# An order held by dependencies: a block kernel's small products and its projections in turn on TensorE

## Chip, cores and metric

The kernel runs on one core of a Trainium2 chip. The metric is the device time of one execution in microseconds (us). Before the change it is 761.18 us, the median of three runs (760.28 to 763.1).

## What is computed

One transformer block on 256 tokens of width 1024 with 256 context tokens, in float32. Cut to what matters here:

```python
hx, hc = modulate(x), modulate(ctx)
px, pc = hx @ w_in, hc @ w_in            # split into q, k, v, hyena, rwkv, lru, gates
att = attention(q, k, v)                 # 8 heads over 2 key/value heads
rw  = rwkv(...)                          # per head, forward and backward:
    # s = s*w - (s @ kk)[:, None]*(kk*a) + v[:, None]*k ;  y = s @ r
hy, lr = hyena(...), lru(...)
x = x + g1 * (merge(gates, att, hy, rw, lr) @ w_out)
x = x + g2 * moe(modulate(x))            # 16 experts, 2 per token
```

The recurrence `s` is what the change is about. The kernel does not step through time: it cuts the 512 tokens (context, then x) into eight chunks of 64, computes all products inside a chunk at once, inverts a triangular matrix per chunk, head and direction, and then walks over the eight chunks.

## The kernel before

The program is written with a framework that orders the work. Each engine executes its own instructions strictly in one fixed order. The program text names an engine for every instruction; at build time a scheduler, which plays the program through with estimated durations, gives each engine among its ready instructions the one that comes first in the program text. Where the text wants another order, it adds a dependency that carries no semaphore and only binds the scheduler: `after(ins, other)` (line 296). A class `_Slots` (line 252) adds such dependencies by itself, so that the first writers of all tiles that share a buffer tag come in program order.

**Projections.** `proj(tile_i, both)` (line 625) computes 128 columns of `w_in` for the x tokens (`both` false) or for context and x. SP loads 512 KB of weights into one of three `raw` buffers; ScalarE rounds each half to `whi`, VectorE subtracts to get `wlo` (`split`, line 616); TensorE accumulates into a `pj` tile (two buffers) three products for each of eight slices: 24 matmuls of 128x128 by 128x256 for x alone, 48 for both. In program order the projections behind the rwkv inputs are LX0 and LX1 (line 850), K (860), V (881), Q0 to Q3 (887), LG0 and LG1 (901); six HY projections and the gates come later.

**Units.** A unit is one direction `d` and one half `i` of the four heads: (0,0), (0,1), (1,0), (1,1) as (i,d), line 837, called units 0 to 3. `unit_keys` (line 738) starts with matmuls of 64x128 by 64x512 (tile `low`), each into an `mm` tile, and then is a chain over ScalarE, VectorE and GpSimd (tanh, scan `L`, exponentials, `kr`, `kd`) that ends in the tile `KN`. `unit_products` (line 794) is TensorE's part: for each of two heads, many 64x64 matmuls of `KN` with `kr` into two `mm` tiles, which VectorE masks into `Xs`, `QX` and (d=1) `AT1`; then eight 128x128 transposes of `KN` in two `mm` tiles, which ScalarE copies to `dn`. `mm` has three buffers (line 338), so the second head's products wait for a mask of the first head's. With d=1 a unit has more of the small products than with d=0.

Before the change all of this stands in one loop ahead of the LX projections:

```python
    for n, u in enumerate(units):
        KNs.append(unit_keys(*u))
        if n:
            unit_products(*units[n - 1], KNs[n - 1])
    unit_products(*units[-1], KNs[-1])
```

So the units come first in program order, and the scheduler puts projection matmuls (LX0, LX1, K, V) wherever a unit's next product isn't ready.

**After the units.** Line 911 on, the TT chain: VectorE transposes `Xs` in four pieces into `TT`, runs 31 steps of two dependent operations (`tq`, `TT`), and transposes back (`VA`, `VB`). It needs the masks of all four units. TensorE then makes 128 small products and the loop over eight steps (line 959), the state being carried from step to step. Attention (`attend`, line 1175), the HY projections, the lru and the first gates (`gate`, line 1229) lie around it, the remaining gates and the merge after it, then the experts.

Of the kernel before, what the change touches and what calls it, by code (L numbers as in the profile page):

```python
# [76 lines left out]
def _consts():  # L77
# [101 lines left out]
T_Q, T_K, T_V, T_HY, T_R, T_RK, T_RV, T_W1, T_A1, T_G1, T_LG, T_LX, T_GT = (  # L179
    0, 4, 5, 6, 12, 14, 16, 18, 19, 20, 21, 23, 25)  # L180
# [112 lines left out]
def body(ctx, tc, I, out, dbg=None, upto=None):  # L293
    nc = tc.nc

    def after(ins, other):
        tc.add_manual_dep(ins.ins, other.ins.name, mybir.DependencyInfo(
            mybir.DependencyClass.NoSync, mybir.DependencyReason.SCHED_ONLY), reason="loads in order")
# [4 lines left out]
    V, A, G, T, SP = (_Eng(e, slots) for e in (nc.vector, nc.scalar, nc.gpsimd, nc.tensor, nc.sync))  # L303
# [36 lines left out]
    def pj():  # L340
        return pj_("pj")

    def mm():
        return mm_("mm")
# [4 lines left out]
    def act(o, i, f=AF.Copy, **k):  # L349
        A.activation(out=o, in_=i, func=f, **k)  # L350

    def stt(o, a, s, b, op0=mul, op1=add, eng=V):
        return eng.scalar_tensor_tensor(out=o, in0=a, scalar=s, in1=b, op0=op0, op1=op1)
# [16 lines left out]
    def mmul(o, l, r, start=True, stop=True, shared=False):  # L370
        return T.matmul(out=o, lhsT=l, rhs=r, start=start, stop=stop, skip_group_check=shared)

    def small(name, shape, bufs=1, p_=cw, dt=F32):
        return slots.tile(p_, [P] + shape, dt, name, name, bufs)
# [5 lines left out]
    ident = small("ident", [128], 1, cp)  # L380
# [11 lines left out]
    def pc(name):  # L392
        o, n = _PV[name]
        return pv[:, o:o + n]
# [9 lines left out]
    def tr(o, i):  # L404
        T.transpose(out=o, in_=i, identity=ident[:i.shape[0], :i.shape[0]])
# [51 lines left out]
    def rawt():  # L457
        return slots.tile(wr_, [P, 1024], F32, "raw", "raw", RAW)
# [70 lines left out]
    hcx = [[slots.tile(hx if s_ else keep, [P, 8, 256], F32R, f"h{s_}{q}", f"h{s_}{q}", 1) for q in range(2)] for s_ in range(2)]  # L529
# [10 lines left out]
    for k in range(2):  # L540
        ada_first(k)
        for j in range(4 * k, 4 * k + 4):
            for s_ in range(2):
                v = 1 - s_
                hi, lo = hcx[s_][0][:, j], hcx[s_][1][:, j]
# [66 lines left out]

    spectrum(0)


    def split(w, hf):

        hi = slots.tile(wp, [P, 512], F32R, "whi", "whi", HI)
        lo = slots.tile(wp, [P, 512], F32R, "wlo", "wlo", HI)
        w = w[:, hf * 512:hf * 512 + 512]  # L620
        act(hi, w)
        tt(lo, w, hi.bitcast(F32), sub)
        return hi, lo

    def proj(tile_i, both):

        w = rawt()
        SP.dma_start(w, I["w_in"][tile_i])
        p = pj()
        for hf in range(2):  # L630
            hi, lo = split(w, hf)
            for s_ in ((0, 1) if both else (1,)):
                o = p[:, s_ * 256:(s_ + 1) * 256] if both else p[:, 0:256]
                for jj in range(4):
                    j = 4 * hf + jj
                    ws = slice(jj * 128, (jj + 1) * 128)

                    mmul(o, hi[:, ws], hcx[s_][0][:, j], j == 0 and s_ == (0 if both else 1), False, both)
                    mmul(o, hi[:, ws], hcx[s_][1][:, j], False, False, both)
                    mmul(o, lo[:, ws], hcx[s_][0][:, j], False, j == 7, both)  # L640
        return p if both else p[:, 0:256]


# [76 lines left out]
    def natural(src, name, big, psa, n=4):  # L720
        o = big(name).rearrange("p (a c) -> p a c", a=4)
        pb = psa()
        for a in range(n):
            tr(pb[:, a * 128:(a + 1) * 128], src[:, a * 128:(a + 1) * 128])
        act(o.rearrange("p a c -> p (a c)"), pb)
        return o

    Vn = b4("Vn").rearrange("p a b -> p (a b)").rearrange("p (t i c) -> p t i c", t=4, i=2)
    for i in range(2):
        pb = mm()  # L730
# [60 lines left out]
        stt(KN4[:, :, 1:3], four(ta), -0.5, four(E3), mul, mul)  # L791
        return KN

    def unit_products(i, d, KN):
        for h in range(2):
            hs = slice(64 * h, 64 * h + 64)
            m = 16 * d + 8 * i + 4 * h
            pc_, px_ = mm(), mm()
            for c8 in range(8):
                c = c8 % 2  # L800
                vs, us = slice(64 * c, 64 * c + 64), slice(64 - 64 * c, 128 - 64 * c)
                kd_, nb_ = (KN[hs, (2 * c8 + q) * 64:(2 * c8 + q) * 64 + 64] for q in (c, 1 - c))
                Kc = Kt(d, i, c8)[hs]
                if c8 < 4:
                    o = slice(c8 * 64, c8 * 64 + 64)
                    mmul(pc_[vs, o], kd_, Kc)
                    mmul(pc_[us, o], *((Kc, nb_) if d else (nb_, Kc)))
                else:
                    k0 = 256 + (c8 - 4) * 128
                    o = slice((c8 - 4) * 128, (c8 - 4) * 128 + 128)  # L810
                    KRc = KR[d][i][hs, k0:k0 + 128]
                    mmul(px_[vs, o], kd_, KRc)
                    if d:
                        mmul(px_[us, o.start:o.start + 64], Kc, nb_)
                        mmul(px_[us, o.start + 64:o.stop], nb_, KRc[:, 64:])
                    else:
                        mmul(px_[us, o], nb_, KRc)
                if d:
                    mmul(pc_[us, 256 + (c8 // 2) * 32:288 + (c8 // 2) * 32], nb_, Kc[:, :32])
            mk = cn(f"mask{d}").rearrange("p (c t) -> p c t", c=2).unsqueeze(1).to_broadcast([P, 2, 2, 64])  # L820
            p4 = px_.rearrange("p (t c q s) -> p t c q s", t=2, c=2, q=2)
            tt(Xs[:, m:m + 2], pc_[:, :256].rearrange("p (t c s) -> p t c s", t=2, c=2), mk)
            tt(Xs[:, m + 2:m + 4], p4[:, :, :, 0], mk)
            if d:
                tt(AT1[:, m - 16:m - 12], pc_[:, 256:384].rearrange("p (t s) -> p t s", t=4),
                   cn("late1").unsqueeze(1).to_broadcast([P, 4, 32]))
            tt(QX[:, d, h, i], px_.rearrange("p (c q s) -> p c q s", c=4, q=2)[:, :, 1],
               cn(f"inc{d}").unsqueeze(1).to_broadcast([P, 4, 64]))
        dn = DN[d][i] = b4("dn").rearrange("p a b -> p (a b)").rearrange("p (c k) -> p c k", c=8)
        for c2 in range(2):  # L830
            pb = mm()
            for c4 in range(4):
                o = (4 * c2 + c4) * 128
                tr(pb[:, c4 * 128:c4 * 128 + 128], KN[:, o:o + 128])
            act(dn[:, 4 * c2:4 * c2 + 4].rearrange("p c k -> p (c k)"), pb)

    units = [(0, 0), (0, 1), (1, 0), (1, 1)]
    KNs = []
    for n, u in enumerate(units):
        KNs.append(unit_keys(*u))  # L840
        if n:
            unit_products(*units[n - 1], KNs[n - 1])
    unit_products(*units[-1], KNs[-1])


    ylr = slots.tile(yp, [P, 2, 256], F32, "ylr", "ylr", 1)
# [2 lines left out]
    for i in range(2):  # L849
        p = proj(T_LX + i, True)  # L850
        xc = o2("xc")
        xcs.append(xc)
        act(xc, p, AF.Identity, scale=lcw[:, 2 + i:3 + i], bias=pc("lcb")[:, i:i + 1])
        x3, p3 = xc.rearrange("p (n t) -> p n t", n=2), p.rearrange("p (n t) -> p n t", n=2)
        stt(x3[:, :, 1:], p3[:, :, :-1], lcw[:, i:i + 1], x3[:, :, 1:])
        stt(x3[:, :, :-1], p3[:, :, 1:], lcw[:, 4 + i:5 + i], x3[:, :, :-1])
        stt(x3[:, :, :-2], p3[:, :, 2:], lcw[:, 6 + i:7 + i], x3[:, :, :-2])


    kp = proj(T_K, True)  # L860
    sq = o2("ksq")
    act(sq, kp, AF.Square)
    kf = o2("kf")
# [7 lines left out]
    def rope(x, t=None):  # L871
        pr = mo()[:, :256]
        mmul(pr, rot, x)
        t = o2("rop")[:, :256] if t is None else t
        tt(t, pr, rps)
        tt(x, x, rpc, eng=G)
        tt(x, x, t, add, eng=G)

    rope(kf[:, 256:])
    vs = o2("vs")  # L880
    act(vs, proj(T_V, True))
    vn = natural(vs, "vn", o2, mo)

    yat = slots.tile(yp, [P, 4, 256], F32, "yat", "yat", 1)
    rqx, rq = small("rqx", [4, 4]), small("rq", [4, 4])
    for i in range(4):
        p = proj(T_Q + i, False)
        sqt, q_ = o2("qsq"), yat[:, i]
        sq = sqt[:, :256]
        act(sq, p, AF.Square)  # L890
        act(q_, p, AF.Copy, scale=pc("q_norm"))
        pq = mo()
        for a in range(2):
            mmul(pq[:, a * 2:a * 2 + 2], sq[:, a * 128:a * 128 + 128], cn("blk2"))
        ts(rqx[:, i], pq[:, :4], 1.0 / 64, EPS)
        rope(q_, sqt[:, 256:])
# [23 lines left out]
    for j in range(31):  # L920
        n, w = 31 - j, j + 1
# [12 lines left out]
    for m in range(32):  # L934
        d, o = m // 16, (m % 16) * 32
# [9 lines left out]
    for m in range(32):  # L945
        d, o = m // 16, (m % 16) * 32
# [20 lines left out]
    for step in range(8):  # L967
# [3 lines left out]
        for d in range(2):  # L971
            c8 = order[d][step]
# [24 lines left out]
        if step < 7:  # L997
# [5 lines left out]
            for h in range(2):  # L1003
                f_ = fch[hv[h], :, :, step:step + 1].to_broadcast([64, 2, 2, 64])
                o = Sn[hv[h], :, :, hv[h]]
# [5 lines left out]
        if step >= 4:  # L1011
            for d, (c8, t_, vs, us, m0, VU) in enumerate(st):
                for i in range(2):
                    o = py[:, i, c8 - 4, :]
# [51 lines left out]
    for c in range(6):  # L1066
        p = proj(T_HY + c, False)
# [684 lines left out]
    with tc.If(over > 0):  # L1752
# [3 lines left out]
        for a in range(2):  # L1756
            hs_ = slots.tile(p2, [P, 8, 128], F32, "yeh", "yeh", 1)
            tt(hs_, h2h[:, a].bitcast(F32), h2l[:, a].bitcast(F32), add)
            for j4 in range(2):
                pt = mb()  # L1760
                for jj in range(4):
                    j = 4 * j4 + jj
# [3 lines left out]
        for e in range(NE):  # L1766
            w13 = [[wload(name, e, q) for q in range(4)] for name in ("w1", "w3")]
            w2_ = [wload("w2", e, q) for q in range(4)]
            for a in range(2):
                as_ = slice(a * 128, a * 128 + 128)  # L1770
                ph = []
                for ws in w13:
                    p = hb()
# [46 lines left out]
```

## Time and profile before

| | |
|---|---|
| median of three runs | 761.18 us |
| profiled execution, its own time | 760.28 us |
| its span, first to last instruction | 758.5 us |
| mean granted TensorE clock | 0.948 |
| TensorE busy (matmuls) | 704.4 us, 93% |
| VectorE busy | 469.4 us, 62% |
| ScalarE busy | 277.2 us, 37% |
| read from HBM | 172.97 MB |

All times of rows are microseconds from the start of the span. PE is TensorE's matmuls, PEld its weight loads, DVE VectorE, ACT ScalarE, POOL GpSimd, SP the engine that issues loads. PEclk is the clock that TensorE was granted, as a share of 2.4 GHz; it is either 1.00 or 0.50 at a time, and other values are means over a stretch. Matmuls overlap, so their durations add to more than the time that passes: the distance from one start to the next is what a matmul costs in a run of them. Every instruction has the line of one helper, L285; they are told apart by their tiles, whose buffer numbers are left out. An f32 matmul shows as two records, an fp32r matmul (projections) and a transpose as one.

### The profile page before, as it was taken

To read this page: it belongs to the slowest core of one execution; us is meant where nothing else is said; L and a number is where in the kernel's file an instruction comes from. 1 tells how busy PE (TensorE), PEld (TensorE's weight loads), DVE (VectorE), ACT (ScalarE), POOL (GpSimd) and SP (SyncE) were. 2 spreads that over 40 slices of the span, in tenths; PEclk is the share of its full clock that TensorE was granted. 3 is DMA by queue.
4 is the path that set the end of the run, shared out by engine and by line. 5 is a ranking of instruction groups with operands and counts; after the bars stand their busy time and mean duration, and the time that the engine had idled before them with its cause. 6 is when DMAs were issued, how large, how long until landed. Compare 5 with 4: busy or idle time off the path is not lost.

```text
span 758.5 us, 13397 instructions
## 1 busy us (share of the span) xinstructions
PE 704.4 (93%) x5109; PEld 493.1 (65%) x5109; DVE 469.4 (62%) x1001; ACT 277.2 (37%) x522; POOL 83.6 (11%) x85
## 2 busy tenths in 40 slices
PE   3989998998998999999999998969999999999996
PEld 1478986797778677777899897865445344343334
DVE  6485467789895677799998577683325215221214
ACT  4362453333353667845445533441111011020101
POOL 0140012112200011000201255010000001000000
PEclk9999995798895999999999999978999999999999
DMA  8761320123432023466797687419999999999995
GB/s 332 280 219 56 111 85 1 29 75 102 127 117 86 1 85 119 153 210 225 237 322 265 246 287 271 138 47 400 408 409 409 408 409 408 410 409 393 409 386 146
DMA packets 53929, 174.97 MB, mean 231 GB/s; under 512 B 5474, under 2 KB 12514, under 8 KB 53858
## 3 DMA queue, kind: packets, MB, share of 16 engines
q1 hardware_dynamic: 50928, 168.79, 61.1%
q10 hardware_dynamic: 2930, 5.25, 1.9%
q8 instruction: 42, 0.69, 0.4%
q14 instruction: 29, 0.24, 0.1%
HBM read 172.97 MB, written 1.05 MB: 229 GB/s over the span
## 4 chain that ended last, share of the span: by engine, by line
PE 71%; DVE 15%; DMA 5%; ACT 4%; issue 3%; POOL 1%; SPq 0%; DVEq 0%; ACTq 0%; POOLq 0%
PE hb L285 25%; PE pj L285 16%; PE mm L285 14%; PE mo L285 11%; PE mb L285 6%; DVE wlo L285 2%; DMA mw<-in_wb_dram 2%; DVE acc L285 2%; DVE TT L285 1%; DVE xt L285 1%; DMA wwA<-in_w_dram 1%; DMA raw<-in_wb_dram 1%; ACT prob L285 1%; DMA rk<-in_rg_dram 1%; DVE h2l L285 1%
## 5 line engine op out<-in xcount | busy, mean ns | idle before, releaser
L285 PE MATMUL pj<-h,whi 128*128 128x256 f32 x1072 | 210.3, 295 | 3.4 <-ACT whi L285 1.8
L285 PEld LDWEIGHTS pj<-h,whi 128*128 128x128 f32 x1072 | 173.7, 197 | 14.2 <-issue 6.4
L285 PE MATMUL pj<-h,wlo 128*128 128x256 f32 x536 | 158.7, 297 | 2.7 <-DVE wlo L285 2.6
L285 ACT ACTIVATE whi<-raw 128x512 fp32r<-128x512 f32 x130 | 81.1, 629 | 118.5 <-PE pj L285 81.9
L285 DVE TENSOR_TENSOR wlo<-raw,whi 128x512 fp32r<-128x512 f32 x130 | 93.7, 730 | 31.7 <-ACT whi L285 31.4
L285 PEld LDWEIGHTS pj<-h,wlo 128*128 128x128 f32 x536 | 105.4, 197 | 8.3 <-DVE wlo L285 4.3
L285 DVE TENSOR_TENSOR act<-act,hb 128x512 f32<-128x512 f32 x8 | 5.5, 687 | 85.4 <-PE hb L285 49.4
L285 PE MATMUL hb<-wwA,g 128*32 128x512 f32 (+2 forms) x180 | 48.5, 594 | 0.0
L285 ACT ACTIVATE yeh<-sct,cw 128x512 fp32r<-128x512 f32 (+2 forms) x19 | 12.1, 652 | 66.0 <-DVE sct L285 65.6
L285 DVE TENSOR_TENSOR sct<-hb,gg 128x512 f32<-128x512 f32 (+2 forms) x19 | 11.3, 606 | 39.6 <-PE hb L285 39.4
L285 PE MATMUL hb<-wwA,aT 128*128 128x512 f32 (+2 forms) x112 | 32.2, 596 | 0.0
L285 PEld LDWEIGHTS hb<-wwA,g 128*32 128x32 f32 (+2 forms) x180 | 16.5, 137 | 23.8 <-issue 22.4
L285 ACT ACTIVATE aT<-mb 128x512 f32<-128x512 f32 x8 | 4.8, 597 | 71.9 <-PE hb L285 44.4
L285 PE MATMUL hb<-wh,g 128*32 128x512 f32 (+2 forms) x84 | 26.8, 615 | 0.0
L285 DVE TENSOR_TENSOR x<-mb,x 128x512 f32<-128x512 f32 (+2 forms) x38 | 21.0, 600 | 9.2 <-PE mb L285 9.2
L285 DVE SCALAR_TENSOR_TENSOR gg<-adaw,sT,gg 128x512 f32<-128x512 f32 x32 | 23.6, 741 | 1.6 <-ACT gg L285 1.5
L285 PE MATMUL hb<-wB,g 128*32 128x512 f32 (+1 forms) x144 | 24.4, 594 | 0.0
L285 PE MATMUL mb<-Dh,h2h 128*128 128x256 f32 (+1 forms) x80 | 20.9, 324 | 3.7 <-DVE Dh L285 3.2
L285 DVE SCALAR_TENSOR_TENSOR acc<-adaw,sT,acc 128x512 f32<-128x512 f32 x32 | 23.8, 773 | 0.0
L285 PEld LDWEIGHTS hb<-wwA,aT 128*128 128x128 f32 (+2 forms) x112 | 11.8, 148 | 17.4 <-issue 16.6
L285 PEld LDWEIGHTS mb<-Dh,h2h 128*128 128x128 f32 x80 | 15.6, 217 | 10.3 <-issue 7.5
L285 ACT ACTIVATE g<-mb,c 128x256 f32<-128x256 f32 (+1 forms) x20 | 9.8, 520 | 33.4 <-PE mb L285 33.4
(482 smaller groups left out, 1390.5 us busy)
## 6 DMA issues: line engine op xcount, KB each, us to landing
wwA<-in_w_dram SPq DMA_DIRECT2D x68, 512.0 KB, 10.1
raw<-in_w_in_dram SPq DMA_DIRECT2D x57, 512.0 KB, 3.9
adaw<-in_ada_dram SPq DMA_DIRECT2D x44, 512.0 KB, 4.9
wB<-in_w_dram SPq DMA_DIRECT2D x38, 512.0 KB, 10.1
wC<-in_w_dram SPq DMA_DIRECT2D x24, 512.0 KB, 10.1
wh<-in_w_dram SPq DMA_DIRECT2D x22, 512.0 KB, 10.1
wD<-in_w_dram SPq DMA_DIRECT2D x18, 512.0 KB, 10.1
wb<-in_w_dram SPq DMA_DIRECT2D x10, 512.0 KB, 10.1
```

What stands on the lines that cost most here:

```text
L285: r = f(*a, **k)
```

## The change

Units 0 and 1 get their keys first. Then the LX projections are made, and from there on a unit's products and a projection take turns. `proj` remembers its last matmul in `proj_end`, and can be told to start `behind` an instruction; `unit_products` binds its first product behind the given matmul and returns its last transpose. The keys of units 2 and 3 are called after the products of units 0 and 1.

```diff
+    proj_end = None
...
-    def proj(tile_i, both):
-
+    def proj(tile_i, both, behind=None):
+
+        nonlocal proj_end
...
-                    mmul(o, hi[:, ws], hcx[s_][0][:, j], j == 0 and s_ == (0 if both else 1), False, both)
+                    first_ = mmul(o, hi[:, ws], hcx[s_][0][:, j], j == 0 and s_ == (0 if both else 1), False, both)
+                    if behind:
+                        after(first_, behind)
+                        behind = None
                     mmul(o, hi[:, ws], hcx[s_][1][:, j], False, False, both)
-                    mmul(o, lo[:, ws], hcx[s_][0][:, j], False, j == 7, both)
+                    proj_end = mmul(o, lo[:, ws], hcx[s_][0][:, j], False, j == 7, both)
...
-    def unit_products(i, d, KN):
+    def unit_products(i, d, KN, behind):
...
-                    mmul(pc_[vs, o], kd_, Kc)
+                    first_ = mmul(pc_[vs, o], kd_, Kc)
+                    if not (h or c8):
+                        after(first_, behind)
...
-                tr(pb[:, c4 * 128:c4 * 128 + 128], KN[:, o:o + 128])
+                last_ = T.transpose(out=pb[:, c4 * 128:c4 * 128 + 128], in_=KN[:, o:o + 128], identity=ident)
             act(dn[:, 4 * c2:4 * c2 + 4].rearrange("p c k -> p (c k)"), pb)
+        return last_
...
-    KNs = []
-    for n, u in enumerate(units):
-        KNs.append(unit_keys(*u))
-        if n:
-            unit_products(*units[n - 1], KNs[n - 1])
-    unit_products(*units[-1], KNs[-1])
+    KNs = [unit_keys(*u) for u in units[:2]]
...
+    done = unit_products(*units[0], KNs[0], proj_end)
+    KNs.append(unit_keys(*units[2]))
+
+
-    kp = proj(T_K, True)
+    kp = proj(T_K, True, done)
...
     rope(kf[:, 256:])
+    done = unit_products(*units[1], KNs[1], proj_end)
+    KNs.append(unit_keys(*units[3]))
     vs = o2("vs")
-    act(vs, proj(T_V, True))
+    act(vs, proj(T_V, True, done))
     vn = natural(vs, "vn", o2, mo)
+    done = unit_products(*units[2], KNs[2], proj_end)
...
     for i in range(4):
-        p = proj(T_Q + i, False)
+        p = proj(T_Q + i, False, done)
+        if i == 1:
+            done = unit_products(*units[3], KNs[3], proj_end)
+        else:
+            done = None
```

## Rows read from the trace of the kernel before

**Rows 1.** Stretches: each engine's busy us (instructions), PEclk, DMA share, GB/s.
```profile
113.83:138.22 24.39, 20.83 (x155) 16.14 (x154) 16.18 (x32) 8.22 (x16) 3.85 (x4) 0.56 0.01 1
113.83:166.70 52.87, 47.84 (x499) 39.54 (x499) 41.18 (x94) 19.57 (x37) 9.97 (x10) 0.77 0.07 21
166.50:232.30 65.80, 57.96 (x376) 51.05 (x374) 61.19 (x146) 28.53 (x56) 9.15 (x10) 0.87 0.38 113
232.30:400.00 167.70, 163.23 (x1536) 130.58 (x1537) 136.93 (x262) 95.79 (x196) 12.54 (x12) 0.96 0.50 166
505.00:758.00 253.00, 239.44 (x1292) 106.21 (x1292) 84.06 (x194) 32.51 (x59) 5.31 (x8) 0.97 0.97 378
```
**Rows 2.** The same view in two stretches of 4 us.
```profile
136.00:140.00 4.00, 4.00 (x45) 3.94 (x42) 2.21 (x8) 0.77 (x3) 0.43 (x1) 0.50 0.01 4
160.00:164.00 4.00, 4.00 (x93) 3.53 (x93) 2.74 (x13) 0.00 (x0) 0.00 (x0) 1.00 0.02 4
```
**Rows 3.** TensorE's timeline: start, us, operation, count, [idle before, whom it waited for].
```profile
115.96 0.52 PE L285 MATMUL mm<-kr,KN 64*64 64x64 f32 x4 [1.90 <-DVE KN L285]
...
130.91 3.77 PE L285 MATMUL mm<-low 64*128 64x512 f32 x4 [1.66 <-ACT dn L285]
...
139.03 0.63 PE L285 MATMUL pj<-h,whi 128*128 128x256 f32 x2
...
139.67 0.63 PE L285 MATMUL pj<-h,whi 128*128 128x256 f32 x2
...
173.27 1.16 PE L285 MATMUL mo<-ident,hrb 128*128 128x128 f32 x8 [2.23 <-DVE hrb L285]
```
**Rows 4.** The chain that ended last, in order of time: an unbroken run of projections.
```profile
66.28 24.96 PE pj L285 x211
```
**Rows 5.** DMA issues: count, KB each, median us to landing.
```profile
raw<-in_w_in_dram SPq DMA_DIRECT2D x57, 512.0 KB, 3.9
```
**Rows 6.** Projection matmuls (tile pj) in two stretches: busy us (count), PEclk, DMA.
```profile
114.07:138.20 24.13, 5.72 (x21) 0.55 0.01 1
166.45:169.05 2.60, 2.60 (x22) 1.00 0.85 217
```
**Rows 7.** TensorE's timeline around the products of unit 2 (d=0).
```profile
147.42 1.98 PE L285 MATMUL mm<-low 64*128 64x512 f32 x4 [0.69 <-ACT dn L285]
149.33 1.56 PE L285 MATMUL mm<-kr,KN 64*64 64x64 f32 x32
150.82 0.39 PE L285 MATMUL pj<-h,wlo 128*128 128x256 f32 x1
151.04 0.40 PE L285 MATMUL pj<-h,whi 128*128 128x256 f32 x2
...
152.32 0.68 PE L285 MATMUL mm<-kr,KN 64*64 64x64 f32 x16
...
154.21 1.09 PE L285 MATMUL mm<-kr,KN 64*64 64x128 f32 x16
155.23 0.66 PE L285 MATMUL mm<-ident,KN 128*128 128x128 f32 x4
```
**Rows 8.** The second head's products of unit 1 (d=1): busy us (count), PEclk, DMA.
```profile
141.94:144.04 2.10, 2.10 (x56) 1.00 0.00 0
```
**Rows 9.** VectorE's timeline: a mask, and the last KN operations of units 1 and 3.
```profile
122.64 0.42 DVE L285 TENSOR_TENSOR Xs<-mm,cst 128x256 f32<-128x256 f32 x1 [2.08 <-PE mm L285]
...
129.02 0.68 DVE L285 SCALAR_TENSOR_TENSOR KN<-ta,E 128x512 f32<-128x512 f32 x1
...
159.47 0.68 DVE L285 SCALAR_TENSOR_TENSOR KN<-ta,E 128x512 f32<-128x512 f32 x1
```
**Rows 10.** VectorE's operations from 166.4 to 234.6 us, grouped: busy us, mean ns, idle before.
```profile
L285 DVE TENSOR_TENSOR wlo<-raw,whi 128x512 fp32r<-128x512 f32 x23 | 16.2, 706 | 2.9 <-ACT whi L285 2.9
L285 DVE TENSOR_TENSOR tq<-TT 128x31 f32<-128x31 f32 (+15 forms) x31 | 12.5, 405 | 0.3
...
L285 DVE TENSOR_TENSOR kf<-mo,kf 128x512 f32<-128x512 f32 x1 | 0.7, 691 | 0.0
```

## The prediction

> **What bounds the kernel now.** I first cut the profile into stretches [rows 1]. The last one, the experts, moves 378 GB/s with the DMA engines 97% busy, and the change does not touch it. It starts when everything before it is done, so a microsecond won earlier is a microsecond of the total unless another limit takes it back. Before it, from 113.8 to 166.7 us, the four units' keys and products run beside projections, at a mean granted clock of 0.77. From 166.5 to 232.3 us VectorE inverts the triangles (the TT chain) and is busy 61.2 of 65.8 us. From 232.3 to 400 us TensorE is busy 163.2 of 167.7 us, first with the eight scan steps, then with gates.
>
> Inside the first stretch I read the clock: 0.50 from 136 to 140 us, 1.00 from 160 to 164 us [rows 2]; over 113.83 to 138.22 the mean is 0.56 while TensorE reads as 85% busy (20.83 of 24.39 us) [rows 1], so busy time hides what is lost. Just before the clock fell TensorE had stood idle 1.90 us waiting for KN; then came products mixed with short runs of projection matmuls, and another 1.66 us wait at 130.91 [rows 3]. At 0.50 (1.2 GHz) projection matmuls start 0.213 us apart (three of them from 139.03 to 139.67) [rows 3], at 1.00 (2.4 GHz) 0.118 us apart (24.96 us for 211) [rows 4].
>
> **Which edits matter.** The order of the unit steps (keys 0, keys 1, products 0, keys 2, products 1, keys 3, products 2, products 3) is the same in both kernels. New is that LX0 and LX1 lie whole before products 0, K whole between products 0 and 1, V between 1 and 2, Q0 and Q1 between 2 and 3. No instruction is added or removed. The projections keep their order among themselves, so SP issues the same weight loads in the same order; a load lands in 3.9 us [rows 5], less than the 5.7 us of one 48-matmul projection, and there are three buffers. The units issue no DMA. So loads cost nothing; if that cover failed, each late one would cost up to 3.9 us.
>
> **The sum up to the end of products 3**, at full clock, from 113.83 us. Projections: 21 matmuls left of LX1 [rows 6], 48 of K, 48 of V, 24 each of Q0 and Q1, 165 x 0.118 = 19.5 us. Products of a unit with d=0: 1.56 + 0.68 + 1.09 = 3.3 us [rows 7], 6.7 for two; with d=1 one half takes 2.10 us [rows 8], so 8.4 for two units. Eight groups of four transposes at 0.66: 5.3. The key matmuls of units 2 and 3, 1.98 each: 4.0 [rows 7]. Three small attention groups (squares, broadcast, rotation) like the 1.16 us one [rows 3]: 3.5. A projection matmul behind a product starts 0.22 us before its successor (150.82 to 151.04) [rows 7] instead of 0.118, so a change of array shape costs 0.10; four blocks have eight changes, 0.8, where before has twelve stretches of products and 24. Together 48.2 us: products 3 would end at 162.0.
>
> The Trainium skill ("TensorEngine Tiling (Array Packing)", § Tiling Modes) says that changing the tiling mode drains TensorE. The rows agree in direction, with 0.10 us. If a drain were as long as a projection matmul's record, 0.28 us (an estimate), the sixteen changes saved would be worth 4.5 us instead of 1.6, which the sum does not use.
>
> **The waits that the change adds.** A product block is not gapless: there are three mm buffers, and the second head's products need one that VectorE has masked out first. Before, K's matmuls lay in those holes: 1.43 us (150.89 to 152.32) and 1.21 us (153.00 to 154.21) in unit 2 [rows 7]. After, everything queued behind a waiting product on TensorE stands: the rest of the block, the next projection, the next keys; and VectorE's masks wait for them. Lower bound 0 (the mask is done while the other buffer fills), upper 2.64 us a block. I take the middle, 1.3, since the mask itself is short but VectorE is often in something else: 5.2 us for four. Products 3 end at 167.2 against 166.7 before; the TT chain gets its input 0.5 us later, bounds 162.0 and 172.6.
>
> Are the keys in time? KN of unit 1 was ready at 129.70, after VectorE had stood 2.08 us for half-clock products [rows 9]. Without that it is ready near 127.6; products 1 are due after LX1 (2.5), block 0 (3.3 + 1.3 + 1.3), K (5.7) and keys 2 (2.0), at 129.9. For the later units a chain takes 12.7 us from key matmul to KN (147.42 to 160.15) [rows 7, 9], and over 18 us lie between block n and block n+2. So TensorE sets the pace; the smallest margin is 2.3 us, at unit 1.
>
> **What is gained instead.** At that point more is done. Before, 22 matmuls of V [rows 6] and all of Q0 and Q1 lay after products 3: 70 x 0.118 = 8.3 us of TensorE, part of it after a 2.23 us wait for hrb [rows 3]. VectorE is the fuller engine in the TT stretch; two wlo (1.4) and kf (0.7) leave it for the stretch before: 2.1 us [rows 10], where VectorE idles 11.7 of 52.9 us [rows 1]. I put the lead's worth at the end between VectorE's 2.1 and TensorE's 8.3 us (it is nothing if later projections slip into the freed places, the second rival). I take the middle, 5.2, since the TT stretch is VectorE's and what follows is TensorE's. Result: 5.2 - 0.5 = 4.7 us. The profiled execution took 760.28 us (span 758.5), 0.9 under the median 761.18; so 755.6 for such a run, 756.5 as a median. Half a percent, about what a measurement of this kernel can tell from no change, is 3.8 us: "same" is 757.4 to 765.0.
>
> **Rivals.**
> *A larger gain* (0.12): the masks are ready in time, blocks wait nothing, products 3 end at 162.0 and the lead counts in full: 4.7 + 8.3 = 13 us, 748. For it: VectorE's idle time. Against: the holes of 2.64 us.
> *Nothing moves* (0.27): the TT chain has 62 short dependent operations of about 0.4 us with other work between them [rows 10]; if Q2, LG and HY work moves up into every freed place, the chain ends when it did: 761. For it: 23 wlo lie so already. The same time follows if the change does not do what it says: the dependencies bind only a block's first product and its last transpose. Against that: a projection's matmuls accumulate into one tile, and the transposes come last in their buffers.
> *Slower* (0.28): the block waits with no projection allowed in between. With the full 2.64 us a block (10.6) TensorE idles so long that the clock falls as it did after the 1.90 us wait [rows 3], and half of the 144 matmuls of K, V, Q0 and Q1 run 0.095 us slower: 6.8. Products 3 end at 162.0 + 10.6 + 6.8 = 179.4, 12.7 us late; less the lead of 5.2 this is 7.5 slower, 769. It decides once waits and slow matmuls together exceed 9.9 us (4.7 + 5.2). Against it: products at full rate kept the clock at 1.00 from 160 to 164 us [rows 2]. The Trainium skill ("TensorE: Matmul & The Clock Gate", § Step-by-step) states that matmuls stay in program order and only weight loads are pulled ahead, which is this rival's mechanism; that the wait for KN held up LX1's matmuls agrees.
>
> **Numbers.** Forecast 0.33, its own range 752 to 757.4. Faster 0.33 + 0.12 = 0.45, same 0.27, slower 0.28. The range 748 to 769 takes in the bounds and the slower case's middle; outside lie more than half of the matmuls slow (up to 776 with all of them) and the rarest gains.
>
> **What would show it.** Right: between 116 and 140 us the clock stays mostly 1.00; the matmuls of K, V, Q0 and Q1 run unbroken near 0.118 us apart; four blocks of 5 to 7 us; the first transpose of the TT chain comes at 165 to 169 us with Q1 done, and the chain is shorter than before by 2 us or more. Wrong: a first transpose after 172 us, half clock in the projections behind the blocks, or a lead at 167 us that is gone by 400 us.

## The result and the profile after

The change makes the kernel slower: 766.79 us (759.62 to 770.61, 10 runs) against 760.73 us (10 runs), ratio 1.0104, 95% interval 1.0064 to 1.0144. The profiled execution took 768.88 us, span 767.1. Against the profiled execution of before (span 758.5) this is 8.6 us, more than the 6.1 between the medians, and milestones of the two traces say where they arise (us from the start of the span). Ratios and mean clocks below leave out executions over 1.5% above the fastest of their kernel; for masks0_first, before_masks_merge_first and before_merge_first these are 12 of the 29 runs of before, so their ratios come out some 0.3% high, and they are compared by median.

| milestone | before | after | later by |
|---|---|---|---|
| first transpose of the TT chain | 166.49 | 187.56 | 21.1 |
| the chain's last transposes begin (VA) | 228.61 | 246.03 | 17.4 |
| copy after the last scan step | 307.67 | 326.94 | 19.3 |
| first activation of the 24 later gates | 350.96 | 334.88 | -16.1 |
| last gate activation | 439.71 | 442.63 | 2.9 |
| first x2 (after merge and w_out) | 493.27 | 501.18 | 7.9 |
| last store of the result issued | 753.86 | 762.39 | 8.5 |

(Eight gates of the first branch come before these 24, in both kernels.) The chain over TT starts 21.1 us late. Most of that comes back: the projections that the new order does early are no longer to be done, the later gates begin 16.1 us earlier and the last one comes 2.9 us late. Then 5.0 us are lost anew between the last gate and x2.

First the stretches of the kernel after; the first row begins with products 0 and ends with TT's start, and the next four cut up its front part. Columns as in [rows 1].

```profile
117.20:187.60 70.40, 59.54 (x572) 50.82 (x571) 46.60 (x105) 23.05 (x44) 14.52 (x15) 0.73 0.18 53
118.90:122.00 3.10, 0.00 (x0) 0.00 (x0) 3.10 (x10) 2.33 (x5) 1.22 (x1) 1.00 0.00 0
122.00:139.00 17.00, 11.89 (x59) 8.49 (x60) 11.88 (x23) 4.95 (x9) 2.72 (x4) 0.50 0.11 31
139.10:145.90 6.80, 6.80 (x86) 6.48 (x87) 5.09 (x9) 3.42 (x6) 2.05 (x3) 1.00 0.30 80
145.90:159.60 13.70, 13.70 (x103) 10.77 (x100) 6.84 (x24) 2.60 (x4) 0.00 (x0) 0.50 0.01 1
442.63:501.18 58.55, 53.79 (x350) 48.74 (x349) 41.87 (x68) 21.97 (x35) 21.14 (x14) 0.94 0.66 236
```

The same view of before, for the first and the last of these stretches:

```profile
117.20:166.70 49.50, 46.36 (x491) 38.63 (x490) 37.81 (x90) 17.59 (x33) 9.18 (x9) 0.76 0.08 23
439.71:493.27 53.56, 50.97 (x350) 46.62 (x349) 38.91 (x66) 19.89 (x33) 18.74 (x13) 1.00 0.68 237
```

TensorE idles 70.40 - 59.54 = 10.9 us ahead of TT in place of 3.1, and is busy 13.2 us longer. Of this stretch, the projections (tile pj), after and before, and then the small matmuls of the attention (tile mo), after and before:

```profile
117.20:187.60 70.40, 23.16 (x146) 21.76 (x145) 4.31 (x6) 3.96 (x8) 0.73 0.18 53
117.20:166.70 49.50, 17.50 (x95) 14.99 (x96) 4.31 (x6) 1.94 (x3) 0.76 0.08 23
...
117.20:187.60 70.40, 6.72 (x34) 5.04 (x34) 2.44 (x7) 0.60 (x1) 0.73 0.18 53
117.20:166.70 49.50, 1.05 (x8) 0.97 (x8) 0.15 (x1) 0.00 (x0) 0.76 0.08 23
```

So 5.7 us go to 51 more projection matmuls (not 70, since in before the last of LX1 still lie in this stretch and in the changed kernel they are done) and 5.7 to the attention; nearly all of the rest are the units' own matmuls. The clock is in all of them: it was 0.50 for 37.7 us of this stretch (122.0 to 139.1, 145.9 to 159.6, 169.8 to 176.7), before for 23.9 (116.7 to 140.6). In the last stretch, from the last gate to x2, TensorE idles 4.8 us in place of 2.6, and the clock falls there too (0.94, before 1.00).

TensorE's timeline after, which answers to [rows 3, 7]:

```profile
117.25 1.64 PE L285 MATMUL mm<-kr,KN 64*64 64x64 f32 x32
123.34 1.12 PE L285 MATMUL mm<-kr,KN 64*64 64x64 f32 x16 [4.45 <-ACT ta L285]
128.23 1.97 PE L285 MATMUL mm<-kr,KN 64*64 64x128 f32 x16 [3.77 <-DVE Xs L285]
130.14 1.97 PE L285 MATMUL mm<-ident,KN 128*128 128x128 f32 x8
132.03 3.78 PE L285 MATMUL mm<-low 64*128 64x512 f32 x4
...
152.39 3.78 PE L285 MATMUL mm<-low 64*128 64x512 f32 x4
...
169.87 1.97 PE L285 MATMUL mm<-kr,KN 64*64 64x128 f32 x16 [2.64 <-DVE Xs L285]
```

Products 0 stand still for 4.45 and 3.77 us, products 2 for 2.64; products 1 and 3 have no such hole. The key matmuls of unit 2 take 3.78 us at the half clock, as they did before (3.77, [rows 3]); those of unit 3, which took 1.98 us in [rows 7], now take 3.78 too (at 152.39).

VectorE's timeline after shows whom products 0 wait for; it answers to [rows 9]:

```profile
118.34 0.72 DVE L285 SCALAR_TENSOR_TENSOR xc<-pj,pv,xc 128x510 f32<-128x510 f32 x1
...
119.27 0.73 DVE L285 SCALAR_TENSOR_TENSOR xc<-pj,pv,xc 128x510 f32<-128x510 f32 x1
...
120.53 1.39 DVE L285 SCALAR_TENSOR_TENSOR xc<-pj,pv,xc 128x508 f32<-128x508 f32 x2
...
122.25 0.74 DVE L285 SCALAR_TENSOR_TENSOR xc<-pj,pv,xc 128x510 f32<-128x510 f32 x1
...
124.18 0.73 DVE L285 SCALAR_TENSOR_TENSOR xc<-pj,pv,xc 128x508 f32<-128x508 f32 x1
...
126.03 1.21 DVE L285 TENSOR_TENSOR KN<-kd,E 128x512 f32<-128x512 f32 x1
127.16 0.68 DVE L285 SCALAR_TENSOR_TENSOR KN<-ta,E 128x512 f32<-128x512 f32 x1
127.77 0.74 DVE L285 TENSOR_TENSOR Xs<-mm,cst 128x256 f32<-128x256 f32 x2
128.43 0.41 DVE L285 TENSOR_TENSOR QX<-mm,cst 128x256 f32<-128x256 f32 x1
```

The first head's products are done at 118.89, but their masks run at 127.77. VectorE is busy all along with work that the new program text puts ahead of them: the six operations on xc, which take LX's result out of PSUM, and the rest of keys 1 down to KN. Of the three mm buffers the first head holds two; the third is keys 1's until ScalarE copies it at 122.62. So the first hole ends with that copy (ta) and the second with the first mask. In before, VectorE took the first mask of products 0 early, ahead of five of the six operations on xc:

```profile
117.47 0.71 DVE L285 SCALAR_TENSOR_TENSOR xc<-pj,pv,xc 128x510 f32<-128x510 f32 x1
...
118.41 0.41 DVE L285 TENSOR_TENSOR Xs<-mm,cst 128x256 f32<-128x256 f32 x1
```

### The profile page after: what moved, and what is told of

Read it like the earlier page. It is cut to its first block, busy times and chain, and to the rows that moved or that the text cites. A ratio compares the mean times of both kernels' runs of the same rounds, so it can differ in the third digit from the quotient of the medians.

```text
span 767.1 us, 13389 instructions
## 1 busy us (share of the span) xinstructions
PE 705.2 (92%) x5109; PEld 493.6 (64%) x5109; DVE 469.4 (61%) x1001; ACT 279.3 (36%) x522; POOL 83.5 (11%) x85
## 4 chain that ended last, share of the span: by engine, by line
PE 74%; DVE 12%; POOL 4%; ACT 4%; DMA 3%; issue 3%; SPq 0%; ACTq 0%; DVEq 0%; POOLq 0%
PE hb L285 25%; PE pj L285 20%; PE mm L285 15%; PE mo L285 10%; PE mb L285 6%; POOL wbl L285 2%; DMA mw<-in_wb_dram 2%; DVE wlo L285 1%; DVE xt L285 1%; DVE acc L285 1%; DMA raw<-in_w_out_dram 1%; DVE L L285 1%; DVE h2l L285 1%; DVE kd L285 1%; DVE xc L285 1%
## 5 line engine op out<-in xcount | busy, mean ns | idle before, releaser
L285 PE MATMUL pj<-h,whi 128*128 128x256 f32 x1072 | 208.1, 293 | 4.5 <-DVE ylr L285 2.0
L285 PE MATMUL pj<-h,wlo 128*128 128x256 f32 x536 | 156.9, 294 | 2.5 <-DVE wlo L285 2.4
L285 DVE TENSOR_TENSOR wlo<-raw,whi 128x512 fp32r<-128x512 f32 x130 | 91.0, 707 | 37.7 <-ACT whi L285 36.9
L285 PE MATMUL hb<-wwA,aT 128*128 128x512 f32 (+2 forms) x112 | 32.5, 596 | 0.0
L285 PE MATMUL mm<-kr,KN 64*64 64x64 f32 (+2 forms) x288 | 18.8, 277 | 10.9 <-DVE Xs L285 6.4
L285 DVE SCALAR_TENSOR_TENSOR acc<-adaw,sT,acc 128x512 f32<-128x512 f32 x32 | 25.5, 828 | 0.6 <-DMA adaw<-in_ada_dram 0.6
L285 PEld LDWEIGHTS mm<-kr,KN 64*64 64x64 f32 x288 | 16.5, 163 | 12.5 <-DVE Xs L285 6.7
```

The costliest lines, as they stand in the source:

```text
L285: r = f(*a, **k)
```

## The experiments

Two theories stood at the start. *Late masks:* VectorE reaches the masks late, TensorE stands, TT starts late, and that is the loss. *Rigid order:* the dependencies themselves cost, since no projection may fill a hole. A third, *loss after the gates*, put it on the merge. After four runs a fourth joined, the *clock*.

Every run gives its span and mean granted clock. Within one kernel the two go together: the changed kernel took 770.61 us at 0.937 and 759.62 at 0.953; before took 763.46 at 0.941 and 753.15 at 0.963. Fitted over 209 runs of all kernels here, with a level for each kernel and one slope, a microsecond at the half clock goes with 0.31 us of span; so 0.01 of the mean clock goes with 2 x 0.01 x 760 x 0.31 = 4.7 us. The Trainium skill ("TensorE: Matmul & The Clock Gate", § Terms) prices time at the half rate at about half of it; the runs show less, and where the rest of the time hides was not tried. The fit does not say how much of this is cause.

Each kernel has one trace. Up to products 0 the kernels of one order do the same work, and still products 0 begin between 115.96 and 119.38 us in the five with the old order and between 116.09 and 118.17 us in the eight with the new; a single milestone carries some 2 to 3 us of such differences.

| kernel | median us | ratio to before, 95% interval | mean clock |
|---|---|---|---|
| before | 760.1 | | 0.952 |
| changed kernel | 766.79 | 1.0104 (1.0064 to 1.0144) | 0.946 |
| text_only | 761.37 | 1.0026 (0.9994 to 1.0059) | 0.947 |
| masks_first | 759.39 | 0.9983 (0.9948 to 1.0019) | 0.951 |
| text_masks_first | 759.21 | 0.9983 (0.9958 to 1.0007) | 0.950 |
| masks0_first | 760.68 | 1.0055 (1.0017 to 1.0094) | 0.950 |
| filled | 763.41 | 1.0029 (1.0004 to 1.0053) | 0.956 |
| merge_first | 763.92 | 1.0033 (1.0001 to 1.0066) | 0.949 |
| masks_merge_first | 756.40 | 0.9948 (0.9916 to 0.9979) | 0.953 |
| before_tt_late | 757.33 | 0.9945 (0.9909 to 0.9982) | 0.959 |
| before_masks_first | 749.04 | 0.9851 (0.9810 to 0.9892) | 0.968 |
| before_masks_merge_first | 750.38 | 0.9920 (0.9880 to 0.9959) | 0.966 |
| before_merge_first | 761.18 | 1.0043 (1.0008 to 1.0079) | 0.953 |

**The order without the dependencies (text_only).** The changed kernel with this taken out:

```diff
-                    if behind:
-                        after(first_, behind)
-                        behind = None
...
-                    if not (h or c8):
-                        after(first_, behind)
```

> The changed kernel without its two order dependencies: only the program text keeps the new order. Rigid order (the dependencies keep projections out of the holes inside a block): with them gone, projection matmuls fill the holes of 4.45 and 3.77 us in products 0, products 3 end near 170 us and the time is that of before, 759 to 763 us. Late masks (the new text puts the next keys' chain and the six xc operations ahead of products 0's masks on VectorE): the masks stay at 127.8 us and later, products 3 end at 183 to 188 us, 764 to 768 us. Loss after the gates (the merge, whatever the front does): 765 to 768 us.

761.37 us, 5.4 us under the changed kernel: the time is the one that rigid order forecast. Its TT chain, though, starts at 183.15 us, as late masks forecast and not near 170. TensorE's timeline of text_only:

```profile
117.16 1.63 PE L285 MATMUL mm<-kr,KN 64*64 64x64 f32 x32
121.31 0.47 PE L285 MATMUL pj<-h,whi 128*128 128x256 f32 x2 [2.52 <-DVE xc L285]
123.25 1.12 PE L285 MATMUL mm<-kr,KN 64*64 64x64 f32 x16 [1.47 <-ACT ta L285]
124.96 0.77 PE L285 MATMUL pj<-h,whi 128*128 128x256 f32 x2 [0.60 <-DVE xc L285]
127.61 1.97 PE L285 MATMUL mm<-kr,KN 64*64 64x128 f32 x16 [1.88 <-DVE Xs L285]
```

Projection matmuls do go into the holes, but four of them, and the first itself waits 2.52 us, for xc: both pj buffers belong to LX until VectorE has read them. The holes are broken up rather than closed (2.52, 1.47, 0.60 and 1.88 us). The first mask runs at 127.14 us, about as late as in the changed kernel, by the new text alone.

**TT late in the kernel of before (before_tt_late).**

```diff
-        ts(rqx[:, i], pq[:, :4], 1.0 / 64, EPS)
+        rqx_op = V.tensor_scalar(out=rqx[:, i], in0=pq[:, :4], scalar1=1.0 / 64, scalar2=EPS, op0=mul, op1=add)
+        if i == 1:
+            q_done = rqx_op
...
-        V.transpose(out=Lq[rows], in_=Xs[rows, :, 1 - q // 2, 32 * (q % 2):32 * (q % 2) + 32].rearrange("p m t -> p t m"))
+        t_ = V.transpose(out=Lq[rows], in_=Xs[rows, :, 1 - q // 2, 32 * (q % 2):32 * (q % 2) + 32].rearrange("p m t -> p t m"))
+        after(t_, q_done)
```

> The kernel of before with TT's four transposes held on VectorE behind the sum-of-squares step of the second query projection, so that the chain over TT starts some 15 to 20 us later (182 to 187 us in place of 166.5) while units, projections and their mixing stay as they were. If the loss of the change goes through TT's late start: the last step ends 15 to 20 us later, part of it is recovered by gates projections that run earlier, and the time is 765 to 769 us. If the loss comes from elsewhere (the rigid order itself, the merge): 760 to 763 us.

This fells the chain of causes that I had started from. VectorE's timeline of before_tt_late:

```profile
180.33 0.17 DVE L285 TENSOR_SCALAR rqx<-mo 128x4 f32<-128x4 f32 x1 [0.24 <-PE mo L285]
180.40 2.03 DVE L285 STREAM_TRANSPOSE TT<-Xs 32x1024 f32<-32x1024 f32 x1
```

The chain starts 13.9 us later than in before, and the kernel is not slower but 0.55% faster (0.9909 to 0.9982), under both forecasts. TensorE has projections to do meanwhile; the last gate comes at 435.87 us, in these two traces 3.8 us earlier than in before. A late TT chain is not the price; holes on TensorE and its clock are.

**The masks early (masks_first, masks0_first, text_masks_first).** The four mask operations of unit_products are raised in the scheduler's priority, of all units or of unit 0 alone:

```diff
+            with tc.high_priority(2000):
                 tt(Xs[:, m:m + 2], pc_[:, :256].rearrange("p (t c s) -> p t c s", t=2, c=2), mk)
...
```

> The changed kernel with the masks of every unit raised in priority, so that VectorE takes those of products 0 between the xc operations and ahead of keys 1's last steps. Late masks: the holes of 4.45 and 3.77 us in products 0 shrink to about 2 us each, TT's first transpose comes at 178 to 183 us in place of 187.6, and the time falls by a third to two thirds of the 6 us lost: 761 to 765 us. Rigid order: a projection still can't fill what is left, TT after 184 us, 765 to 768 us. Loss after the gates: 765 to 768 us.

> The changed kernel with the masks of unit 0 alone raised in priority. If the loss sits in products 0 (holes of 4.45 and 3.77 us) and what follows from them, nearly all of the gain of raising all masks (766.8 to 759.4 us) is kept: 759 to 762 us. If the 2.64 us hole of products 2 and the later units matter as much: 762 to 765 us.

> The changed kernel's text without its order dependencies, with the masks raised. Without the masks the dependencies cost 0.8% (766.8 against 761.4 us). If they cost only where a late mask leaves a hole that a projection might fill, they cost next to nothing once the masks are early: 757 to 760 us, as with them (759.4). If the strict order costs by itself: 753 to 756 us.

TensorE's timeline of masks_first:

```profile
116.09 1.65 PE L285 MATMUL mm<-kr,KN 64*64 64x64 f32 x32
119.83 1.12 PE L285 MATMUL mm<-kr,KN 64*64 64x64 f32 x16 [2.10 <-DVE Xs L285]
121.24 1.97 PE L285 MATMUL mm<-kr,KN 64*64 64x128 f32 x16 [0.29 <-DVE QX L285]
```

The holes of products 0 shrink from 4.45 and 3.77 us to 2.10 and 0.29, TT starts at 171.92 us, and the time is 759.39 us: more than the third to two thirds of the loss that I had expected, all of it. Unit 0's masks alone bring it to 760.68, so most of what early masks give lies in products 0. And with the masks early the dependencies cost nothing (759.39 with them, 759.21 without; 5.4 us with late masks). The dependencies by themselves are not what costs; they make TensorE stand where a mask is late. VectorE's order in masks_first differs from that in the changed kernel only up to 170 us, so nothing further on was rearranged by the edit.

**The same edit in the kernel of before (before_masks_first).**

> The kernel of before with the masks raised in priority in the same way. Late masks: here the masks of products 0 wait less to begin with (2.08 us of idle VectorE ahead of one of them), so TT comes at most 3 us earlier than 166.5 us and the time is 758 to 761 us. If the place of the masks on VectorE is of no account in either order, 760 to 762 us.

It did far more than either forecast: 749.04 us (6 runs), ratio 0.9851 (0.9810 to 0.9892), the fastest kernel here. Its windows, from products 0 to TT and on to the scan steps:

```profile
113.00:165.50 52.50, 49.08 (x549) 41.87 (x548) 44.37 (x99) 22.05 (x42) 16.20 (x11) 0.90 0.18 51
...
229.82:400.00 170.18, 166.41 (x1611) 134.49 (x1612) 144.71 (x271) 99.99 (x201) 14.64 (x13) 1.00 0.54 180
```

TT starts at 165.50, only 1.0 us earlier than in before. But the clock is 0.90 in the first of these stretches, where it was 0.77 over 113.83 to 166.70 [rows 1], and 1.00 in the second, where it was 0.96. Over its runs the clock is 0.968 against 0.952: 1.6 x 4.7 = 7.5 of the 11 us.

Two things follow. Early masks take the loss away and do not take away the difference of the two orders: with them in both, the new order is 10 us behind (759.39 and 749.04), without them 6.1. And here the edit is not local: aligned with before, some 350 of VectorE's 1002 operations stand elsewhere in its order, up to 430 us. How much of the 11 us the masks themselves bring is not shown.

**The holes filled with work that nothing needs (filled).** The changed kernel with 13 extra matmuls; no mask, no order is touched:

```diff
+                if not (i or d) and (h, c8) in ((0, 7), (1, 3)):
+                    pf = mo()
+                    for _ in range(7 if c8 == 7 else 6):
+                        mmul(pf[:, :256], ident, KN[:, :256])
```

> The changed kernel with 13 extra matmuls of 128x256 (0.59 us each at full clock in the rows of the changed kernel) that nothing reads, put into the two holes of products 0: seven into the one of 4.45 us, six into the one of 3.77 us. It only adds work on TensorE. Clock theory (holes are followed by stretches at half clock, and across the runs so far a kernel's time goes with 0.35 us for each us at half clock): products 0 end at most 1 us later, the stretches at half clock between 122 and 160 us, 30.7 us in all, shrink by 10 us or more, and the time falls to 760 to 764 us. Waits alone (the clock is of no account, only the holes are): 766 to 769 us, since the holes hold the extra work and nothing else moves.

TensorE's timeline of filled:

```profile
117.02 1.56 PE L285 MATMUL mm<-kr,KN 64*64 64x64 f32 x32
118.50 3.29 PE L285 MATMUL mo<-KN,ident 128*128 128x256 f32 x14
123.01 0.68 PE L285 MATMUL mm<-kr,KN 64*64 64x64 f32 x16 [1.22 <-ACT ta L285]
123.62 2.86 PE L285 MATMUL mo<-KN,ident 128*128 128x256 f32 x12
127.37 1.09 PE L285 MATMUL mm<-kr,KN 64*64 64x128 f32 x16 [0.89 <-DVE Xs L285]
128.39 1.09 PE L285 MATMUL mm<-ident,KN 128*128 128x128 f32 x8
```

And its windows, over what were the holes and K in the changed kernel:

```profile
118.50:142.00 23.50, 20.90 (x216) 17.33 (x214) 20.19 (x43) 10.49 (x20) 7.31 (x6) 1.00 0.14 45
```

TensorE waits for the same ScalarE copy and the same mask, but does something meanwhile, and the clock stays at 1.00 up to 142.1 us. (The next stretch at half clock, 13.7 us, stays: 142.1 to 155.8 us in place of 145.9 to 159.6.) The products after the wait take 1.09 us in place of 1.97, TT starts at 181.15 in place of 187.56, and useless work makes the kernel 3.4 us faster, as the clock theory forecast: 763.41 us, ratio 1.0029 (1.0004 to 1.0053) against 1.0104 (1.0064 to 1.0144). The mean clock rises from 0.946 to 0.956, worth 4.7 us by the fit; the extra work gives back a part. That these holes cost through the clock is shown by this run: the waits alone would have left the time where it was, and no rearrangement explains it, for VectorE runs the same operations in the same order but for one swap of neighbours, ScalarE and GpSimd without any. The profiled execution is not the proof of the gain: it took 769.08 us, the longest of the 12. It led the changed kernel's by 4.9 us up to the 28th of the 32 gates (425.38 against 430.32 us) and lost 4.0 of them by the last one, with TensorE waiting 0.93 and 1.39 us for ScalarE and VectorE and another fall of the clock.

**The merge (merge_first, masks_merge_first, before_merge_first, before_masks_merge_first).** The four loads of merge's weights go through one buffer, mw. Their rows, for before, the changed kernel and merge_first (first and last start in us):

```profile
L285 SPq DMA_DIRECT2D mw<-in_wb_dram x4: 327/328/371, 397.0 to 420.0; - x4
```

```profile
L285 SPq DMA_DIRECT2D mw<-in_wb_dram x4: 327/350/423, 387.4 to 440.3; - x4
```

```profile
L285 SPq DMA_DIRECT2D mw<-in_wb_dram x4: 327/328/328, 384.1 to 410.3; - x4
```

The last load goes out 19.5 us ahead of the first merge matmul in before, 2.1 us ahead in the changed kernel, where one VectorE split of the first load came late in VectorE's order (412.61 us) and the second load stood behind others on SP. The edit raises load, rounding copy and splits of these weights:

```diff
+                with tc.high_priority(2000 if n_ < 2 else 0):
                     w = mraw("mw") if n_ < 2 else rawt()
...
```

> The changed kernel with the weights of merge's first two branches (load, rounding copy, two splits) raised in priority, so that the last of their four loads is issued some 30 us ahead of the first merge matmul in place of 2.1 us. Merge theory (5.0 of the 8.5 us between the profiled runs arise between the last gate and x2, because those loads come late): this stretch shrinks from 58.6 us to 53 to 55 us, and the time to 761 to 763 us. If the stretch is paced by VectorE's and GpSimd's own work there, or if the earlier splits only delay gates: 765 to 768 us.

> The changed kernel with both: masks raised, and the weights of merge's first two branches raised. If front and merge are separate losses, the gains add: 759.4 us (masks alone) less the 4 to 5 us of the merge, 754 to 757 us. If the merge's loss is only the front's handed on, the second part adds nothing: 758 to 760 us.

> The kernel of before with the weights of merge's first two branches raised, the control for the same edit in the changed kernel (766.8 to 763.9 us). Merge theory: before has 2.6 us of idle TensorE in this stretch and issues the last of the four loads 19.5 us ahead of the merge, so nothing is to be had: 759 to 761 us. If the edit helps whatever the order: 757 to 758 us.

> The kernel of before with all masks raised (749.0 us) and the weights of merge's first two branches raised. In that kernel the stretch from the last gate to x2 has 2.4 us of idle TensorE already, so that the merge theory expects next to nothing: 747 to 750 us. If early merge weights are worth 3 us whatever the front does: 745 to 747 us. If the earlier loads and splits delay the gates: 751 to 754 us.

The window of merge_first from the last gate to x2:

```profile
440.91:495.90 54.99, 52.48 (x350) 47.95 (x349) 39.62 (x66) 19.88 (x33) 19.25 (x13) 0.97 0.65 231
```

The stretch falls from 58.55 to 54.99 us, TensorE's idle time in it from 4.8 to 2.5, and the time by 2.9 us to 763.92, a little less than forecast (the intervals of the two ratios just touch). With the masks early it is worth 3.0 us as well (759.39 to 756.40), though there the intervals overlap. The stretch itself is clearer: in the six traces of the new text without this edit it takes 58.4 to 59.0 us, whatever the front does, and in the two with it 54.99 and 54.96. So this is a loss of its own and not the front's handed on. In the kernel of before, with late or early masks, the edit brings nothing (760.74 in the same set and 761.18; 749.04 and 750.38).

## Why the prediction was wrong

**Direction and size.** Forecast was 756.5 us, range 748 to 769, with 0.28 for slower; it came out 766.79, inside the range, on the side of the slower rival and 2 us under that rival's 769. That closeness is luck: the rival had TT 12.7 us late and a lead of 5.2 to set against it, where 21.1 and 18.2 were measured, and the merge not at all.

**The step that failed first: the waits that the change adds.** I took 1.3 us a block, 5.2 for four, 10.6 at most. Measured: 8.22 us in products 0, 2.64 in products 2, none in products 1 and 3; 10.9 us, just over the bound. The size is the lesser fault. I read the holes of unit 2 [rows 7] as those of any block and wrote that "the mask itself is short but VectorE is often in something else", without asking what stands ahead of the mask in VectorE's order once the text is moved: xc and keys 1. I had counted the moved step's work on TensorE and on SP, not on VectorE. Nor had I seen that keys 1 hold the third mm buffer, so that the longer hole ends with ScalarE's copy and not with a mask.

**The step that failed by more: the sum at full clock.** It has 48.2 us of work from 113.83 us to the end of products 3. From there to TT's start TensorE was busy 62.87 us:

```profile
113.83:187.56 73.73, 62.87 (x599) 54.06 (x599) 49.83 (x108) 25.86 (x49) 15.75 (x17) 0.75 0.17 51
```

TT came 20.4 us after the forecast 167.2; 14.7 of these are in the work and 5.7 in the waits. Half of the front was not at full clock: K took 7.45 us in place of 5.7, and the key matmuls of units 2 and 3 3.78 each in place of 1.98. Over its three stretches at half clock TensorE was busy 32.5 us; at 1.09 us for 1.97, the products' times in filled and here, full clock would have saved 14.5, an estimate. In before 23.9 us of the front ran at half clock, and the forecast took them as gone. I had given the half clock to the slower rival only, though the 1.90 us wait of [rows 3] and the fall behind it stood in the trace. That rival had the mechanism right, its place (every block) wrong.

**Keys in time: right, by luck.** KN of unit 1 was ready at 127.8 us, as forecast (127.6), but block 0 took 14.9 us where I had 5.9, so nothing waited for it.

**Hand-over to TT.** I had 0.5 us late, the rival 12.7; measured 21.1. My bound of 172.6 held the waits almost in full (10.6 of 10.9), but no half clock, and 3.5 us for the small matmuls of the attention, which took 6.72.

**The lead's worth: larger than I took, and what I subtracted from it did not count.** The chain over TT itself became 3.6 us shorter (58.5 from first transpose to VA in place of 62.1), as forecast ("2 us or more"); but it takes 59.5 to 60.5 us in the other seven traces of the new text and 59.1 to 60.9 in the other four of the old, so this is not clear of what one trace differs from the next. Of the 21.1 us, 18.2 had come back by the last gate, where I had put the lead at 5.2, 8.3 at most. The reason lies in the step "TT gets its input 0.5 us later", which I charged in full to the end: before_tt_late shows that 13.9 us of it cost nothing, because TensorE goes on with gates. What counts is TensorE's idle time and clock wherever they fall. From 113 us to the last gate TensorE idled 19.4 us in before (326.71 less 307.28 busy) and 24.0 in the changed kernel (329.63 less 305.66); these 4.5 us more are where the 2.9 us left at the gates belong:

```profile
113.00:439.71 326.71, 307.28 (x2714) 257.65 (x2714) 265.51 (x532) 166.04 (x328) 40.53 (x38) 0.92 0.43 141
113.00:442.63 329.63, 305.66 (x2721) 257.89 (x2721) 262.92 (x531) 167.02 (x328) 38.58 (x36) 0.91 0.42 136
```

**What I had not seen.** 5.0 of the 8.5 us between the profiled executions arise in the merge, which no step of the prediction touched: the new text delayed a VectorE split and three loads more than 200 us behind the moved step. merge_first shows 2.9 us of it.

**Loads, and array shapes.** Loads cost nothing, as forecast: no block or projection of the front waited for raw. A change of array shape at 0.10 us could not be seen beside these terms.

**What would show it wrong** did show it: a first transpose after 172 us, half clock in the projections behind the blocks, and a lead gone by 400 us (the eighth of the 24 later gates at 389.98 us against 387.70, where the first of them led by 16.1).

**What stays open.** Not every hole is followed by a fall of the clock: in before_masks_first TensorE idled 2.52 us at 192.4 us and the clock stayed at 1.00, while during the 2.10 us hole of masks_first it fell, to 0.50 from 119.1 to 132.8 us. Which holes cost is not settled, and so neither is why the two orders, both with early masks, stand 10 us apart (759.39 and 749.04): the clock's 0.951 and 0.968 go with 8 of them, and the merge, by masks_merge_first, with some 3, part of which is clock too.

## What to carry to other kernels

When program text moves, follow what it now precedes on every engine, not only on the one that the change is about: here six VectorE operations on xc and the rest of keys 1 went ahead of a few short masks, and TensorE stood 8.2 us. A strict order on one engine is only as good as the latest operand from another; with the masks raised the dependencies cost nothing. Try a remedy in the kernel of before as well: there the same edit gained 1.5%, more than it gave the new order. Before pricing a delay, ask whether the engine that sets the end has other work meanwhile: 14 us on the chain over TT cost nothing, while 8 us without work on TensorE cost time and clock.

## What the runs showed that I had not expected

Useless matmuls made a kernel faster (13 of them, 3.4 us), because the clock then stayed at 1.00 over what had been 17 us at 0.50.

The clock also fell without a hole: in the windows of the changed kernel TensorE is busy 6.80 of 6.80 us from 139.10 to 145.90 at 1.00, in K and the dense products 1, and then runs 13.7 us at 0.50, again busy throughout. The Trainium skill ("TensorE: Matmul & The Clock Gate", § What's actually happening) says that the gate follows how busy the engine has been of late; a busy engine in this sense of the profile was slowed all the same.
